# A decoder layer on one core: array shapes kept apart, GpSimd without arithmetic, softmax on turned scores

## The chip, the core and the metric

The kernel runs on one core of one Trainium2 chip. The metric is device microseconds of one execution. Three runs of the kernel before took 632.46, 633.56 and 633.76 us; their median is 633.56. A core has TensorE (matrix products), VectorE, ScalarE and GpSimd (elementwise work), and SyncE, which here issues all transfers. Each engine carries out its own instructions in the order in which the program lists them, and waits on semaphores for the others.

## The reference

One layer of a decoder for 512 tokens and 1024 channels. After an RMS norm, one projection gives the inputs of two token mixers and two merge gates. Branch A is causal attention with 8 heads of 64 channels and a relative-position bias (with 512 tokens every past block is selected, so all past keys count). Branch B is an RWKV-7 time mix, also 8 heads of 64 channels. The gated merge is followed by an output projection, a second RMS norm, and a gate that adds a per-layer embedding.

```python
u = _rms_norm(h, g_pre[i]);  cols = u @ w_in[i]
# A: softmax(q k' / 8 + bias[q_pos - k_pos], past keys only) @ v, times silu(z_A)
# B, for every token t and head (S is 64 x 64):
sa = einsum('bhvk,bhk->bhv', S, a_t)
S = S * w_t + sa b_t' + v_t k_t';   y_t = S r_t
# group norm of y, bonus, times silu(z_B)
merged = sigmoid(gate_a) * (y_a @ p_a) + sigmoid(gate_b) * (y_b @ p_b)
h = h + _rms_norm(merged @ w_out, g_post)
h = h + sigmoid(h @ w_ple_gate) * (p @ w_ple_up)
```

All inputs and the output are float32.

## The kernel before

Activations lie with channels on the 128 partitions and the 512 tokens along the free axis. A large product `w x` is made of three passes in the type float32r over a high and a low part of each operand: `wh xh + wh xl + wl xh`. Each pass is a TensorE instruction with a 128 x 128 weight tile and up to 512 columns; `product()` issues 24 of them for 8 tiles of input channels. Weights arrive in tiles of 128 x 1024 (`raw`). ScalarE makes the high part (`whi`), and VectorE or GpSimd subtracts it to make the low part (`wlo`); for the projections of the first phase every other tile goes to GpSimd (`weights()`, line 371).

The work has these stages. The start, to about 75 us, splits x, computes the norm and makes the first four projections. From then to about 480 us three things run at the same time. `fill()` makes the other projections in the order of the string `FILL`; its products are the `pp<-u_hi,whi` rows. `rwkv(j)` does the recurrence for four pairs of heads j one after the other: vectors and decays first, then the Gram products (`g<-W,BK`), the inverses of unit triangular matrices by doubling (`inverse()`, rows `Z`, `X`, `Xt`), and the chain over 8 chunks of 64 tokens. `attention()` does four pairs of heads: scores in `psc`, softmax, transposes in `ptp`, products with v. After that follow the merge, the output projection, the post-norm and the embedding gate.

Within the chain a chunk goes TensorE (`p_rhs`, rows `c<-SV,W`), ScalarE (`rh`), TensorE (`c<-rh,AT`), ScalarE or VectorE (`SV<-c`), TensorE (`p_s`), VectorE (`SV<-c,D,sd`), and so to the next chunk. The output `p_y` (rows `y<-SV,W`) is issued after the update. It has four products: for each of two heads one with 64 rows (`W1`, the old state) and one with 128 rows (`W2`, the new values), all with 64 weight columns. The head decides which half of the output partitions they write. The group norm of a pair ends with `y<-cst,Y`, which turns the result.

The scores (lines 1203 to 1207) take two products per head and query tile: `QS` with its high and low parts above each other on 128 rows times the high part `KH`, and the 64 rows with the high part of q times the low part `KL`. The up projections of decay and rate (lines 967 to 970) have the same form: 128 rows, then 64 rows with `wa_lo`. The softmax keeps two float16 parts of the probabilities (`ph`, `pl`), and the transposes are two float16 products per block of 128 x 128 against a scaled identity.

The order of instructions is not written out. The class `Plan` interleaves the streams at build time: every instruction is given a rough price in `Engine.price`, and the stream whose next step can start first goes on; recurrence and attention have a small bonus. So a price decides the order on every engine, and nothing at run time does. For TensorE the price is the number of columns with an allowance for the weight load, and 0.022 us for a product that runs beside its predecessor.

Of the kernel before, what the change touches and what calls it, by code (L numbers as in the profile page):

```python
# [35 lines left out]
T = 512  # L36
# [6 lines left out]
PSCALE = 16384.0  # L43
# [77 lines left out]
class Stream:  # L121
    """A sequence of instructions that yields the engine of its next step, or ("wait", mark)."""
# [101 lines left out]
class Engine:  # L224
    """An engine whose instructions are also priced in the plan."""
# [4 lines left out]

    def price(self, name, out, args, kw):
        """Microseconds, roughly."""
        n = math.prod((args[0] if name == "tensor_reduce" else out).shape[1:])
        if self.key == "P":
            m = args[0].shape[1]
            wide = out.dtype == F32 and args[0].dtype == F32
            four = args[0].dtype in (F32, F32R)
            load, d = ((4 * m, 4 * n) if wide else (2 * m, n) if four else (m // 4, n))
            load, d = max(0.0, load / 2400 - self.plan.streamed) if m > 64 else 0.0, d / 2400
            pos = out.base_partition() if m <= 64 else None  # L240
            beside = pos is not None and self.last is not None and pos != self.last
            self.last = None if beside else pos
            self.plan.streamed = 0.022 if beside else d
            return 0.022 if beside else load + d + 0.0025
# [34 lines left out]
class Queue:  # L279
    """The queue of the transfers, which are priced as well."""  # L280
# [15 lines left out]
def hybrid_kernel(ctx: ExitStack, tc, xT, pT, wu, wda, wmain, wpab, wout, wpg, vec_in, cst_in, oneh, relb, wupa,  # L296
# [47 lines left out]
    # weight tiles: their loads and splits run ahead of the products, those of the last two matrices in extra places  # L344
# [18 lines left out]
    def weights():  # L363
        for i, name in enumerate(order):
# [11 lines left out]
            eng = pool if i % 2 and name[0] not in "mow" else dve  # L376
# [12 lines left out]
    def product(name, ps, mh, ml, kts, cols=FULL, done=True, pace=None):  # L389
        """Adds w x over the k tiles kts = (of w, of x) on the given tokens."""  # L390
# [17 lines left out]
    def rsqrt(y, x, t):  # L408
        """y * RS = x ** -0.5 for x > 0: an integer seed, a step of Newton's kind and one of the third order."""
# [26 lines left out]
    def token_rstd(parts_, scale, eps, half, res):  # L436
        """[128, 256] of 1/sqrt(scale * column sums of the parts + eps), the same on every partition, in PSUM."""
# [30 lines left out]
    id16s = main.tile([128, 128], F16, name="id16s")  # L468
# [10 lines left out]
    # operands of the up projections of decay and rate, high and low parts above each other  # L479
    wd_x, ad_x, wd_w, ad_w, wa_lo = (main.tile([128, 512], F32R, name=n) for n in ("wd_x", "ad_x", "wd_w", "ad_w", "wa_lo"))  # L480
# [41 lines left out]
    def setup():  # L522
# [34 lines left out]
        dve.tensor_scalar(id16s, ident, 1.0 / PSCALE, None, op0=OP.mult)  # L557
# [27 lines left out]
    def first_split(i, q):  # L585
        ks = slice(2 * q, 2 * q + 2)
        yield ("wait", f"dw{i}")
        yield "A"
        act.activation(sw[i][0][:, ks], sraw[i][:, ks], AF.Copy)
        eng = pool if i or q else dve  # L590
        yield eng.key
        eng.tensor_tensor(sw[i][1][:, ks], sraw[i][:, ks], sw[i][0][:, ks].bitcast(F32), op=OP.subtract)
        plan.mark(f"f{i}{q}")

    def up_weights(w, there):
        plan.at(there)
        for a, b, d in ((lo_, hi_, wd_w), (hi_, lo_, ad_w)):
# [5 lines left out]
            dve.tensor_tensor(wa_lo[a], w[a], d[a].bitcast(F32), op=OP.subtract)  # L603
# [103 lines left out]
    def norm_split(kt, uf):  # L707
        yield "A"
        act.activation(u_hi[:, kt, :], uf, AF.Copy)
        yield "G" if kt % 2 else "D"  # L710
        (pool if kt % 2 else dve).tensor_tensor(u_lo[:, kt, :], uf, u_hi[:, kt, :].bitcast(F32), op=OP.subtract)
        plan.mark(f"u{kt}")

    def bias_lines():
        yield ("wait", "u7")
        for q in range(2):
# [3 lines left out]
            act.activation(line[:, 320 * q:320 * q + 320], ps[0:8, 0:320], AF.Copy)  # L720
# [12 lines left out]
    def statics():  # L733
        """The recurrence takes the place of the start."""
# [44 lines left out]
    def evacuate(i, w, j, ps):  # L779
# [15 lines left out]
        elif w == "Q":  # L795
            q = QS[j] = at.tile([128, 2, T], F32R, tag="qs", name="qs")
            for h, a, b in ((0, lo_, hi_), (1, hi_, lo_)):
                yield "A"
                act.activation(q[a, h, :], ps[a], AF.Copy, scale=0.125)
                dve.scalar_tensor_tensor(q[b, h, :], ps[a], 0.125, q[a, h, :].bitcast(F32), op0=OP.mult,  # L800
                                         op1=OP.subtract)
        elif w == "K":
            kh = KH[j] = at.tile([128, 2, T], F32R, tag="kh", name="kh")
            kl = KL[j] = at.tile([128, T], F32R, tag="kl", name="kl")
            for h, a, b in ((0, lo_, hi_), (1, hi_, lo_)):
# [3 lines left out]
                dve.tensor_tensor(kl[a, :], ps[a], kh[a, h, :].bitcast(F32), op=OP.subtract)  # L809
# [50 lines left out]
    def inverse(j, q, Ah, Al, AT, Xt, X):  # L860
        """The inverses of the unit triangular matrices of four chunks."""
# [74 lines left out]
    def rwkv(j):  # L936
# [8 lines left out]
        # 1 / |k * k_k| per token and head  # L945
# [18 lines left out]
        # log decays and in-context rates  # L964
        yield "P"
        pw, pa = bank(), bank()
        for ps, w, x, lo in ((pw, wd_w, wd_x, lo_), (pa, ad_w, ad_x, hi_)):
# [14 lines left out]
        # their sums from the middle of each chunk on, at 65 points; E = their exponentials  # L982
# [25 lines left out]
        # operands of the chunks: W1 = [a | L v part, r, identity, a of the second head], BK = [b, k]  # L1008
# [25 lines left out]
        def w1(eng, cs):  # L1034
# [500 lines left out]
```

## Time and profile before

| what | value |
|---|---|
| runs | 632.46, 633.56, 633.76 us |
| profiled execution, first to last instruction (the page gives no other time of it) | 635.5 us, 10491 instructions |
| TensorE, products | busy 615.8 us (97%), 3992 |
| TensorE, weight loads | 470.7 us (74%) |
| VectorE | 450.7 us (71%), 1003 |
| ScalarE | 310.2 us (49%), 695 |
| GpSimd | 105.5 us (17%), 87 |
| TensorE's mean granted clock | 0.983 |
| transfers | 64.51 MB, mean 102 GB/s |

The profile is of one execution. In its views PE is TensorE, PEld its weight loads, DVE VectorE, ACT ScalarE, POOL GpSimd. All instructions carry line 263, because one helper records them; the names of the tiles tell them apart (result first, then what is read). A matmul's duration includes its way through the array, so matmuls overlap and the distance from start to start is what one costs. A float32 product of 64 columns appears as two records.

### The profile page before, as it was taken

What the parts mean: (1) busy time and instruction counts of PE and PEld (TensorE: products, weight loads), DVE (VectorE), ACT (ScalarE), POOL (GpSimd) and SP (SyncE); (2) the same over time, 40 slices, a digit from 0 to 9 for tenths busy, and PEclk for the clock granted to TensorE, in tenths of its full rate; (3) what the DMA queues carried; (4) which work ended last, traced back from release to release, by engine and by line L of the source; (5) the groups of instructions that cost most, each with busy time, mean ns of one, the idle gap of its engine ahead of it and who ended that gap; (6) DMA issues with size and microseconds to landing.
All of it is one profiled execution on the core that took longest, in us unless ns stands there. A gap on an engine that the chain in (4) does not pass through costs nothing.

```text
span 635.5 us, 10491 instructions
## 1 busy us (share of the span) xinstructions
PE 615.8 (97%) x3992; PEld 470.7 (74%) x3992; DVE 450.7 (71%) x1003; ACT 310.2 (49%) x695; POOL 105.5 (17%) x87
## 2 busy tenths in 40 slices
PE   7999999999999999999999999999999999999997
PEld 4878777667776767676777666776778888898986
DVE  6987787876768878667977867675585766469533
ACT  7555264555455455446465354654463336444312
POOL 4531331101112110112111012201010001014100
PEclk9999999999999999799899999999999999999999
DMA  8315621112212121111210301221165555820211
GB/s 309 122 60 211 203 99 64 36 68 101 76 47 77 35 85 59 59 66 47 88 51 34 134 34 50 84 84 50 52 215 209 180 178 182 297 92 25 100 51 50
DMA packets 26210, 64.51 MB, mean 102 GB/s; under 512 B 2695, under 2 KB 7303, under 8 KB 25904
## 3 DMA queue, kind: packets, MB, share of 16 engines
q1 hardware_dynamic: 26160, 63.85, 28.8%
q8 instruction: 31, 0.51, 0.3%
q14 instruction: 19, 0.16, 0.1%
HBM read 55.69 MB, written 10.77 MB: 105 GB/s over the span
## 4 chain that ended last, share of the span: by engine, by line
PE 82%; DVE 13%; ACT 2%; issue 1%; DMA 1%; SPq 0%; DVEq 0%; ACTq 0%
PE pp L263 44%; PE s L263 12%; PE g L263 11%; PE c L263 8%; PE y L263 7%; DVE xl L263 2%; DVE BK L263 1%; DVE W L263 1%; DMA x_sb<-xT 1%; DVE tv L263 1%; DVE pr L263 1%; DVE xh L263 1%; DVE Y L263 1%; DVE mean L263 1%; DVE ph L263 0%
## 5 line engine op out<-in xcount | busy, mean ns | idle before, releaser
L263 PE MATMUL pp<-u_hi,whi 128*128 128x512 f32 x360 | 150.9, 419 | 0.0
L263 PE MATMUL pp<-u_hi,wlo 128*128 128x512 f32 x360 | 149.2, 414 | 0.0
L263 PE MATMUL pp<-u_lo,whi 128*128 128x512 f32 x360 | 148.4, 412 | 0.0
L263 POOL TENSOR_TENSOR wlo<-raw,whi 128x1024 fp32r<-128x1024 f32 (+1 forms) x29 | 60.5, 2093 | 319.2 <-ACT whi L263 313.4
L263 ACT ACTIVATE whi<-raw 128x1024 fp32r<-128x1024 f32 (+1 forms) x86 | 71.4, 846 | 30.9 <-PE pp L263 24.1
L263 PEld LDWEIGHTS pp<-u_hi,wlo 128*128 128x128 f32 x360 | 68.7, 191 | 15.0 <-issue 1.5
L263 PEld LDWEIGHTS pp<-u_lo,whi 128*128 128x128 f32 x360 | 68.7, 191 | 15.0 <-issue 2.0
L263 PEld LDWEIGHTS pp<-u_hi,whi 128*128 128x128 f32 x360 | 68.8, 191 | 14.2 <-issue 1.4
L263 DVE TENSOR_TENSOR wlo<-raw,whi 128x1024 fp32r<-128x1024 f32 (+1 forms) x57 | 52.8, 937 | 10.1 <-ACT whi L263 9.8
L263 PEld LDWEIGHTS y<-SV,W 64*64 64x64 f32 (+1 forms) x256 | 24.4, 134 | 15.6 <-issue 8.8
L263 PE MATMUL y<-SV,W 64*64 64x64 f32 (+1 forms) x256 | 35.4, 246 | 0.0
L263 ACT ACTIVATE rh<-c 128x64 f32<-128x64 f32 x29 | 6.5, 224 | 53.8 <-PE c L263 53.6
L263 ACT ACTIVATE SV<-c 64x64 f32<-64x64 f32 (+2 forms) x63 | 19.3, 306 | 23.0 <-DVE SV L263 14.0
L263 DVE SCALAR_TENSOR_TENSOR SV<-c,D,sd 64x64 f32<-64x64 f32 x56 | 15.8, 283 | 16.4 <-PE c L263 11.5
L263 PE MATMUL c<-SV,W 128*64 128x64 f32 x240 | 22.8, 243 | 3.6 <-ACT SV L263 2.9
L263 PEld LDWEIGHTS c<-SV,W 128*64 128x64 f32 x240 | 14.5, 136 | 15.1 <-ACT SV L263 8.2
L263 ACT ACTIVATE P<-P,sml 128x128 f32<-128x128 f32 (+3 forms) x32 | 17.9, 561 | 7.3 <-DVE sml L263 7.2
L263 PE MATMUL g<-W,BK 64*128 64x192 f32 x128 | 16.5, 360 | 4.2 <-DVE W L263 4.2
L263 DVE SCALAR_TENSOR_TENSOR pl<-P,sml,ph 128x128 f16<-128x128 f32 (+3 forms) x32 | 19.7, 615 | 1.1
L263 ACT ACTIVATE sd<-SV,D 64x64 f32<-64x64 f32 x56 | 19.1, 341 | 0.8
L263 PEld LDWEIGHTS g<-W,BK 64*128 64x128 f32 x128 | 11.7, 194 | 9.2 <-issue 8.9
L263 DVE CUSTOM_DVE_ANT_0 P<-s,bt 128x128 f32<-128x128 f32 (+3 forms) x32 | 15.5, 485 | 3.6 <-PE s L263 3.0
(372 smaller groups left out, 1401.3 us busy)
## 6 DMA issues: line engine op xcount, KB each, us to landing
raw<-wmain SPq DMA_DIRECT2D x48, 512.0 KB, 3.2
g_dram<-gst SPq DMA_DIRECT2D x16, 256.0 KB, 2.0
raw<-wpab SPq DMA_DIRECT2D x8, 512.0 KB, 3.3
raw<-wout SPq DMA_DIRECT2D x8, 512.0 KB, 3.7
raw<-wpg SPq DMA_DIRECT2D x8, 512.0 KB, 5.2
bb_dram<-b_dram SPq DMA_DIRECT2D x1, 2560.0 KB
x_sb<-xT SPq DMA_DIRECT2D x4, 512.0 KB, 5.0
bt<-bb_dram SPq DMA_DIRECT2D x8, 256.0 KB, 3.6
```

The costliest lines, as they stand in the source:

```text
L263: r = f(out, *args, **kw)
```

## The change

Three parts of it concern what TensorE is given. `KL` gets a second half: 128 rows with the low part of k on both halves, so that the second score product reads all 128 rows of `QS`. The up projections get low-part weights with 128 rows (`wd_l`, `ad_l`). The four products of `p_y` are issued in another order: first the two with 128 rows, one per head, then the two with 64 rows.

The planner's price for TensorE is replaced by `array()`. It knows the shape of the array that a product uses, and adds a price when the shape or the type changes.

GpSimd loses all its subtractions and products to VectorE (weight splits, `W1`'s second half, `yn`, `u_lo`, `h_lo`, `wul`, `pl` of the embedding); only memsets stay there. The softmax works on scores with the sign turned: q is scaled by -0.125 and the bias line by -1, the reduction takes a minimum, and the exponential has scale -1, so the negated maximum is there at once. The probabilities stay in float32 in `P`, the parts `ph` and `pl` go, and one float32 transpose takes the place of two float16 products. A scratch area for transfers issued elsewhere is made smaller.

```diff
 class Engine:
+    def array(self, name, out, w, n):
+        k, m = w.shape[0], math.prod(w.shape[1:])
+        if name == "transpose":
+            m = k
+        cut = lambda a: 32 if a <= 32 else 64 if a <= 64 else 128
+        mode, kind = (cut(k), cut(m)), w.dtype
+        each = lambda s: max(0.025, s / 2400 + 0.0025)
+        if kind == F32:
+            d = each(2 * n) if name == "transpose" else 2 * each(2 * n)
+        else:
+            d = n * 0.455e-3 if kind == F32R else each(n)
+        last = self.last
+        spot = w.base_partition(), out.base_partition()
+        full = (128, 128)
+        beside = lambda a, b: (mode[0] < 128 and a[0] != b[0]) or (mode[1] < 128 and a[1] != b[1])
+        if last is not None and last[0] == mode != full and all(beside(spot, s) for s in last[2]):
+            last[2].append(spot)
+            return 0.012
+        if last is not None and last[0] != mode:
+            d += 0.09 if last[1] == F32R else 0.045
+        if last is not None and kind == F32R and mode == full and (last[0] != full or last[1] != F32R):
+            d += 0.085
+        self.last = mode, kind, [spot]
+        self.plan.streamed = d
+        return d
...
-            eng = pool if i % 2 and name[0] not in "mow" else dve
+            eng = dve
...
-                act.activation(q[a, h, :], ps[a], AF.Copy, scale=0.125)
+                act.activation(q[a, h, :], ps[a], AF.Copy, scale=-0.125)
...
-            kl = KL[j] = at.tile([128, T], F32R, tag="kl", name="kl")
+            kl = KL[j] = at.tile([128, 2, T], F32R, tag="kl", name="kl")
...
-                dve.tensor_tensor(kl[a, :], ps[a], kh[a, h, :].bitcast(F32), op=OP.subtract)
+                dve.tensor_tensor(kl[a, h, :], ps[a], kh[a, h, :].bitcast(F32), op=OP.subtract)
+                yield "A"
+                act.activation(kl[b, h, :], kl[a, h, :].bitcast(F32), AF.Copy)
...
-            pe.matmul(ps, wa_lo[lo, jc], x[lo], start=False, stop=True)
+            pe.matmul(ps, low[:, jc], x, start=False, stop=True)
...
-                pe.matmul(p_y[lo_], W1[lo_, c, 1, :], SV[lo_, c, 0, 0, :], start=True, stop=False)
-                pe.matmul(p_y[lo_], W2[:, c, 0, 0:64], SV[:, c, 0, 1, :], start=False, stop=True)
-                pe.matmul(p_y[hi_], W1[hi_, c, 1, :], SV[hi_, c, 1, 0, :], start=True, stop=False)
-                pe.matmul(p_y[hi_], W2[:, c, 1, 0:64], SV[:, c, 1, 1, :], start=False, stop=True)
+                pe.matmul(p_y[lo_], W2[:, c, 0, 0:64], SV[:, c, 0, 1, :], start=True, stop=False)
+                pe.matmul(p_y[hi_], W2[:, c, 1, 0:64], SV[:, c, 1, 1, :], start=True, stop=False)
+                pe.matmul(p_y[lo_], W1[lo_, c, 1, :], SV[lo_, c, 0, 0, :], start=False, stop=True)
+                pe.matmul(p_y[hi_], W1[hi_, c, 1, :], SV[hi_, c, 1, 0, :], start=False, stop=True)
...
-        dve.tensor_tensor_reduce(P, psc, bt[:, T - n:T], 1.0, NEG, op0=OP.add, op1=OP.max, accum_out=mx)
-        dve.tensor_scalar(nm, mx, -1.0, None, op0=OP.mult)
+        dve.tensor_tensor_reduce(P, psc, bt[:, T - n:T], 1.0, -NEG, op0=OP.add, op1=OP.min, accum_out=nm)
...
-        act.activation(P, P, AF.Exp, bias=nm, accum_out=sm_)
+        act.activation(P, P, AF.Exp, bias=nm, scale=-1.0, accum_out=sm_)
...
-        dve.tensor_scalar(ri, ri, PSCALE, None, op0=OP.mult)
-        dve.tensor_scalar(ph, P, ri, None, op0=OP.mult)
-        dve.scalar_tensor_tensor(pl, P, ri, ph, op0=OP.mult, op1=OP.subtract)
+        dve.tensor_scalar(P, P, ri, None, op0=OP.mult)
...
-                        pe.matmul(psc[h][:, c], QS[j][rows, h, q], KL[j][rows, 0:n], start=False, stop=True)
+                        pe.matmul(psc[h][:, c], QS[j][:, h, q], KL[j][:, h, 0:n], start=False, stop=True)
...
-                        pe.matmul(ptp[h][:, c], ph[h][:, c], id16s, start=True, stop=False)
-                        pe.matmul(ptp[h][:, c], pl[h][:, c], id16s, start=False, stop=True)
+                        pe.transpose(ptp[h][:, c], P[h][:, c], ident)
```

## Rows read from the trace of the kernel before

**Rows 1.** The page: busy time, share of the span and instructions of each engine.
```profile
PE 615.8 (97%) x3992; PEld 470.7 (74%) x3992; DVE 450.7 (71%) x1003; ACT 310.2 (49%) x695; POOL 105.5 (17%) x87
```

**Rows 2.** The page: chain of work that ended last, shares of the span by engine.
```profile
PE 82%; DVE 13%; ACT 2%; issue 1%; DMA 1%; SPq 0%; DVEq 0%; ACTq 0%
```

**Rows 3.** TensorE's waits: who waited for whom, us in total, times, longest.
```profile
PE c L263 <- ACT SV L263: 2.9, 2, 1.5
```

**Rows 4.** Timeline of TensorE from 197 us (start, us, engine, what): score products.
```profile
197.06 0.33 PE L263 MATMUL s<-kh,qs 128*128 128x128 f32 x1
...
199.34 0.51 PE L263 MATMUL pp<-u_hi,whi 128*128 128x512 f32 x1
199.68 0.40 PE L263 MATMUL pp<-u_lo,whi 128*128 128x512 f32 x1
199.91 0.40 PE L263 MATMUL pp<-u_hi,wlo 128*128 128x512 f32 x1
```

**Rows 5.** Timeline of TensorE: y and the next chunk's first products.
```profile
175.79 1.04 PE L263 MATMUL y<-SV,W 64*64 64x64 f32 x7
...
176.94 0.50 PE L263 MATMUL pp<-u_lo,whi 128*128 128x512 f32 x1
```

**Rows 6.** Timeline of TensorE: a pair on 128 rows and 64 columns.
```profile
144.81 0.34 PE L263 MATMUL c<-SV,W 128*64 128x64 f32 x4
145.07 0.50 PE L263 MATMUL pp<-u_hi,wlo 128*128 128x512 f32 x1
```

**Rows 7.** Timeline of TensorE: eight pairs on 64 x 64, in brackets the wait before.
```profile
302.12 1.15 PE L263 MATMUL y<-cst,Y 64*64 64x64 f32 x32 [1.26 <-DVE Y L263]
303.20 0.51 PE L263 MATMUL pp<-u_lo,whi 128*128 128x512 f32 x1
```

**Rows 8.** Timeline of TensorE: the four up projections of one pair of heads.
```profile
79.20 0.40 PE L263 MATMUL g<-wd_x,wd_w 128*128 128x512 f32 x1
...
80.82 0.51 PE L263 MATMUL pp<-u_lo,whi 128*128 128x512 f32 x1
```

**Rows 9.** Timeline of TensorE: four float32 transposes.
```profile
296.81 0.60 PE L263 MATMUL pp<-cst,vc 128*128 128x128 f32 x4
297.24 0.49 PE L263 MATMUL c<-cst,vb 128*128 128x128 f32 x3
```

**Rows 10.** Timeline of TensorE: first and last of sixteen float16 products.
```profile
149.21 0.23 PE L263 MATMUL s<-id16s,ph 128*128 128x128 f16 x1
...
150.06 0.22 PE L263 MATMUL s<-id16s,pl 128*128 128x128 f16 x1
```

**Rows 11.** Groups by shape: busy us, mean ns, idle before; weight splits of both engines.
```profile
L263 POOL TENSOR_TENSOR wlo<-raw,whi 128x1024 fp32r<-128x1024 f32 x22 | 54.8, 2493 | 312.7 <-ACT whi L263 307.0 <-PE s L263 5.7
L263 DVE TENSOR_TENSOR wlo<-raw,whi 128x1024 fp32r<-128x1024 f32 x36 | 43.9, 1221 | 7.6 <-ACT whi L263 7.2
```

**Rows 12.** The page's costliest groups: the softmax's low part.
```profile
L263 DVE SCALAR_TENSOR_TENSOR pl<-P,sml,ph 128x128 f16<-128x128 f32 (+3 forms) x32 | 19.7, 615 | 1.1
```

**Rows 13.** Timeline of VectorE from 371 us.
```profile
372.46 2.77 DVE L263 TENSOR_TENSOR BK<-kka,En 128x512 f32<-128x512 f32 x1
375.15 0.68 DVE L263 TENSOR_TENSOR BK<-fk,En 128x512 f32<-128x512 f32 x1
```

**Rows 14.** Timeline of GpSimd, same stretch.
```profile
372.27 2.41 POOL L263 TENSOR_TENSOR wlo<-raw,whi 128x1024 fp32r<-128x1024 f32 x1 [23.02 <-ACT whi L263]
```

**Rows 15.** Timeline of TensorE, same stretch.
```profile
376.93 0.34 PE L263 MATMUL c<-SV,W 128*64 128x64 f32 x4 [1.51 <-ACT SV L263]
```

**Rows 16.** Busy time by stretch, granted clock third from last: first and last of three.
```profile
262.60:272.80 10.20, 10.20 (x28) 6.85 (x29) 5.14 (x10) 6.75 (x13) 0.00 (x0) 0.50 0.01 2
...
378.70:382.00 3.30, 3.30 (x14) 2.60 (x12) 1.04 (x3) 1.77 (x3) 0.00 (x0) 0.50 0.00 0
```

**Rows 17.** One tile's instructions: duration min/median/max in ns, first and last start.
```profile
L263 PE MATMUL y<-cst,Y x128: 218/218/267, 200.2 to 474.4; 64*64 64x64 f32 x128
```

**Rows 18.** Busy time by stretch (span, PE, PEld, DVE, ACT, POOL, clock), middle part.
```profile
75.00:475.00 400.00, 389.94 (x2777) 281.06 (x2776) 296.92 (x731) 210.37 (x498) 64.10 (x37) 0.98 0.20 70
```

More of the change, by code (lines that the diff above doesn't have):

```diff
@@ L42 @@
 GN_EPS = 64e-5
-PSCALE = 16384.0
 DECAY = math.exp(-0.5)
@@ L234, in price @@
         if self.key == "P":
[L235 to L244, printed above, removed]
+            return self.array(name, out, args[0], n)
         if name == "memset":
@@ L477, in shift_mix @@
         dve.scalar_tensor_tensor(o, ps, omu[:, col:col + 1], m[:, 0:T], op0=OP.mult, op1=OP.add)
-    wd_x, ad_x, wd_w, ad_w, wa_lo = (main.tile([128, 512], F32R, name=n) for n in ("wd_x", "ad_x", "wd_w", "ad_w", "wa_lo"))
+    wd_x, ad_x, wd_w, ad_w, wd_l, ad_l = (main.tile([128, 512], F32R, name=n)
+                                          for n in ("wd_x", "ad_x", "wd_w", "ad_w", "wd_l", "ad_l"))
     hw0 = main.tile([128, 4], F32, name="hw0")
@@ L589, in first_split @@
         act.activation(sw[i][0][:, ks], sraw[i][:, ks], AF.Copy)
-        eng = pool if i or q else dve
-        yield eng.key
-        eng.tensor_tensor(sw[i][1][:, ks], sraw[i][:, ks], sw[i][0][:, ks].bitcast(F32), op=OP.subtract)
+        yield "D"
+        dve.tensor_tensor(sw[i][1][:, ks], sraw[i][:, ks], sw[i][0][:, ks].bitcast(F32), op=OP.subtract)
         plan.mark(f"f{i}{q}")
@@ L596, in up_weights @@
         plan.at(there)
-        for a, b, d in ((lo_, hi_, wd_w), (hi_, lo_, ad_w)):
+        for a, b, d, low in ((lo_, hi_, wd_w, wd_l), (hi_, lo_, ad_w, ad_l)):
             yield "A"
@@ L602, in up_weights @@
             yield "D"
-            dve.tensor_tensor(wa_lo[a], w[a], d[a].bitcast(F32), op=OP.subtract)
+            for half in (a, b):
+                dve.tensor_tensor(low[half], w[a], d[a].bitcast(F32), op=OP.subtract)
         plan.mark("up")
@@ L709, in norm_split @@
         act.activation(u_hi[:, kt, :], uf, AF.Copy)
-        yield "G" if kt % 2 else "D"
-        (pool if kt % 2 else dve).tensor_tensor(u_lo[:, kt, :], uf, u_hi[:, kt, :].bitcast(F32), op=OP.subtract)
+        yield "D"
+        dve.tensor_tensor(u_lo[:, kt, :], uf, u_hi[:, kt, :].bitcast(F32), op=OP.subtract)
         plan.mark(f"u{kt}")
@@ L719, in bias_lines @@
             pe.matmul(ps[0:8, 0:320], rb_, oh[:, 320 * q:320 * q + 320], start=True, stop=True)
-            act.activation(line[:, 320 * q:320 * q + 320], ps[0:8, 0:320], AF.Copy)
+            act.activation(line[:, 320 * q:320 * q + 320], ps[0:8, 0:320], AF.Copy, scale=-1.0)
         sp.dma_start(b_dram, line)
@@ L966, in rwkv @@
         pw, pa = bank(), bank()
-        for ps, w, x, lo in ((pw, wd_w, wd_x, lo_), (pa, ad_w, ad_x, hi_)):
+        for ps, w, low, x in ((pw, wd_w, wd_l, wd_x), (pa, ad_w, ad_l, ad_x)):
             yield "P"
             pe.matmul(ps, w[:, jc], x, start=True, stop=False)
-            pe.matmul(ps, wa_lo[lo, jc], x[lo], start=False, stop=True)
+            pe.matmul(ps, low[:, jc], x, start=False, stop=True)
         Ep = rw.tile([128, NCH, 65], F32, name="Ep")
@@ L1032, in rwkv, with w1 @@
         ep3 = Ep[:, :, 1:65]
-        def w1(eng, cs):
-            yield "G" if eng is pool else "D"
-            eng.tensor_tensor(W1[:, cs, 1, :], r3[:, cs], ep3[:, cs], op=OP.mult)
-            yield "G" if eng is pool else "D"
-            eng.tensor_tensor(W1[lo_, cs, 0, :], kn3[lo_, cs], Ep[lo_, cs, 0:64], op=OP.mult)
-            yield "G" if eng is pool else "D"
-            eng.tensor_tensor(W1[hi_, cs, 3, :], kn3[hi_, cs], Ep[hi_, cs, 0:64], op=OP.mult)
+        def w1(cs):
+            yield "D"
+            dve.tensor_tensor(W1[:, cs, 1, :], r3[:, cs], ep3[:, cs], op=OP.mult)
+            yield "D"
+            dve.tensor_tensor(W1[lo_, cs, 0, :], kn3[lo_, cs], Ep[lo_, cs, 0:64], op=OP.mult)
+            yield "D"
+            dve.tensor_tensor(W1[hi_, cs, 3, :], kn3[hi_, cs], Ep[hi_, cs, 0:64], op=OP.mult)
             plan.mark(f"w1{j}.{cs.start}")
-        plan.spawn(w1(pool, slice(4, 8)), BR)
-        yield from w1(dve, slice(0, 4))
+        yield from w1(slice(0, 4))
+        plan.spawn(w1(slice(4, 8)), BR)
         yield "P"
@@ L1154, in rwkv @@
         yield ("wait", f"z{j}")
-        eng = pool if j < 3 else dve
-        yield eng.key
-        eng.tensor_tensor(yn, yn, bv, op=OP.add)
-        yield eng.key
-        eng.tensor_tensor(yn, yn, ZZ[j], op=OP.mult)
+        yield "D"
+        dve.tensor_tensor(yn, yn, bv, op=OP.add)
+        yield "D"
+        dve.tensor_tensor(yn, yn, ZZ[j], op=OP.mult)
         if j < 3:
@@ L1164, in rwkv, with softmax @@
         plan.mark(f"post{j}")
[L1166 to L1169 removed]
+    def softmax(h, P, psc, bt, n, name):
+        sml = at.tile([128, 3], F32, tag="sml", name="sml", bufs=4)
+        nm, sm_, ri = (sml[:, i:i + 1] for i in range(3))
         yield "D"
[L1171 to L1172 removed]
+        dve.tensor_tensor_reduce(P, psc, bt[:, T - n:T], 1.0, -NEG, op0=OP.add, op1=OP.min, accum_out=nm)
         yield "A"
[L1174 removed]
+        act.activation(P, P, AF.Exp, bias=nm, scale=-1.0, accum_out=sm_)
         yield "D"
         dve.reciprocal(ri, sm_)
[L1177 to L1179 removed]
+        dve.tensor_scalar(P, P, ri, None, op0=OP.mult)
         plan.mark(name)
@@ L1199, in attention @@
                 psc = [bank(f"s{h}", 1) for h in range(2)]
-                P, ph, pl = ([at.tile([128, T], d, tag=f"{t}{h}", name=t) for h in range(2)]
-                             for t, d in (("P", F32), ("ph", F16), ("pl", F16)))
+                P = [at.tile([128, T], F32, tag=f"P{h}", name="P") for h in range(2)]
                 for h, rows in heads:
@@ L1409, in h_split @@
         act.activation(hi[:, n, c], x[:, n, c], AF.Copy)
-        yield "G" if n % 2 else "D"
-        (pool if n % 2 else dve).tensor_tensor(lo[:, n, c], x[:, n, c], hi[:, n, c].bitcast(F32), op=OP.subtract)
+        yield "D"
+        dve.tensor_tensor(lo[:, n, c], x[:, n, c], hi[:, n, c].bitcast(F32), op=OP.subtract)
         plan.mark(f"h{n}.{h}")
```

20 lines of the change are left out of this document (7 added, 13 removed).

## The prediction

> **What bounds the kernel now.** I began with the page's busy shares: TensorE is busy for 97% of the span [rows 1], and the chain that ended last gives it 82% and VectorE 13% [rows 2]. A busy TensorE is not yet one that streams, since matmuls overlap, so the next view was its timeline, read from start to start. Between two large products of 512 columns with nothing else around the starts lie 0.23 us apart, as at 199.68 and 199.91 [rows 4]. That is 0.45 ns a column, and it is the yardstick for all that follows: what a stretch takes above it is the cost of something other than streaming. Two such costs stand out. Whenever a product uses another part of the array than the one before it (64 rows or 64 columns in place of 128), the starts move apart [rows 4 to 8]. And VectorE is sometimes held for two microseconds beside a GpSimd instruction, after which TensorE waits [rows 13 to 15]. The waits as such are short: 2.9 us in all for the chain's products [rows 3], 1.26 us for one group norm [rows 7]. So from about 75 us on the kernel is bound by what TensorE is given to do, with the recurrence, whose norms come 91 us apart (four bursts from 200.2 to 474.4) [rows 17], as a serial path beside it that is nearly as long.
>
> **Low parts of the scores on 128 rows.** The eight score products of two heads run from 197.06 to 199.34, that is 2.28 us, for 2 x 2 x (128 + 256) = 1536 columns, which stream in 1536 x 0.45 = 0.69 us [rows 4]. The excess of 1.59 us belongs to the four products with 64 rows: 0.40 us each, for going to the other shape and back. With `KL` on 128 rows the shape doesn't change, and the streaming stays as it is (columns count, not rows). There are 4 pairs x 2 heads x 4 query tiles = 32 of them: 12.7 us. From below I set half of it (6.4), should a short product of 128 columns not reach the yardstick. On this the Trainium skill has a rule in "TensorE: Matmul & The Clock Gate", section LDWEIGHTS: loading weights takes the number of their columns divided by 1.2, about 107 ns for 128, and by its section on weight-path modes float32 gets no faster path. By that rule the 16 products with 128 columns (0.06 us of streaming) would last some 0.05 us longer each, an estimate from that page, and the sum would be 0.8 us higher; no row of before has such a product between others of its own shape.
>
> The copies that fill the second half of `KL` are 8 ScalarE instructions of 64 x 512. ScalarE is busy 49% [rows 1]; they delay a pair's first scores by well under a microsecond and I cost them at nothing, 0 to 2.4 us if scores were what ended a stage.
>
> **Up projections on 128 rows.** Four products take 79.20 to 80.82 = 1.62 us, where four of 512 columns stream in 0.92 [rows 8]: 0.70 us, once for each of 4 pairs, 2.8 us. The two additional subtractions come once, early, on VectorE: below 1.5 us, and not waited for there.
>
> **y in pairs of heads.** Now a chunk's four products change shape each time: with the next chunk's first product pair behind them they take 175.79 to 176.94 = 1.15 us [rows 5]. Afterwards they are three pairs, each in one shape. A pair on 128 rows and 64 columns takes 0.26 us with the change behind it [rows 6]. Of a pair on 64 x 64 eight in a row take 1.08 us, 0.14 each [rows 7]; alone it is between this and the 0.26 of the other pair, and I take 0.26, because it too is followed by a change. 3 x 0.26 = 0.78, so 0.37 us are saved, in 32 chunks 11.8 us. Ends: 0.25 to 0.50 a chunk (8 to 16 us).
>
> **Float32 transposes.** Four existing ones go from 296.81 to 297.24, 0.11 us each [rows 9]. What they replace: 16 float16 products in 15 steps from 149.21 to 150.06, 0.057 us each, two to a block [rows 10], so 0.113. Nothing, in 80 blocks, give or take 1 us. Signs turned in scale factors cost nothing.
>
> **No arithmetic on GpSimd.** Its 105.5 us [rows 1] go to VectorE, which does the same split of 128 x 1024 in 1.22 us instead of 2.49 [rows 11]: about half, some 51 us. VectorE loses the 19.7 us of `pl` [rows 12] and 64 short instructions. What it also loses are the holds: `BK<-kka,En` takes 2.77 us where a like instruction right behind takes 0.68 [rows 13], while GpSimd is in a 2.41 us split [rows 14]; the chain's update stood behind it, and TensorE then waited 1.51 us [rows 15]. Each of the 22 splits there [rows 11] can hold one instruction for 2.77 - 0.68 = 2.1 us, which is 0 to 46 us; I take half, 23, of which some 20 fall between 75 and 475 us. So 51 - 20 - 23 - the short ones leaves next to nothing: VectorE, busy 297 of these 400 us [rows 18], should stay near that.
>
> The granted clock was at its lower level, 1.2 GHz, in three stretches, the first of 10.2 and the last of 3.3 us [rows 16], some 16.8 us together, of which half is lost: 8.4 us. Before each of them TensorE had just waited 1.3 to 1.5 us, the last two times as in rows 7 and 15. With the waits (2.9 + 1.3) there are 12.6 us that hang on held instructions. VectorE's order stays strict, and a split can still stand before the chain; I take 8 of them (0 to 12.6).
>
> **The order.** The planner prices TensorE anew, by shape changes that the trace shows, so all engines get a new order, and every queue's instructions move against each other. It cannot be read from the profile. Each return to the large products costs 0.34 instead of 0.23 us, as from 199.34 to 199.68 [rows 4]; with 70 interruptions more or fewer, a guess at a third of them, that is 8 us either way, and I take nothing. The transfers are issued by SP as before; the smaller scratch space for transfers issued elsewhere costs nothing.
>
> **Sum.** 12.7 + 2.8 + 11.8 + 8 = 35.3; 635.5 - 35.3 = 600.2. The profiled execution is 1.9 us above the median of the runs, which would make 598. Can the recurrence follow? It must lose 35.3 / 4 = 8.8 us in each of its 91 us. It has 8 x 0.37 = 3.0 from y, which stands before the next chunk's product; up to 20 / 4 = 5.0 from holds; some of the 3.2 from the scores that it queues behind; 2 from the clock. With two thirds of that, 9, it just does. For this narrow margin I leave the 2 us in and say 600, with 590 to 610 as this case's own range.
>
> **Rivals.**
> 1. The recurrence becomes the bound. For: it is serial, and nearly as long as TensorE's work now. Against: TensorE hardly waits for it now [rows 3]. If it gains only the y pairs and the up projections, 3.7 us a period, 14.8 in all, the time is 635.5 - 14.8 = 621, whatever TensorE saves.
> 2. The new order interrupts the large products more often, 140 times rather than 70: 140 x 0.11 = 15 us, so 615. For: nothing in the change makes the planner prefer to stay in a shape; it only prices the change. Against: priced right, it fits fewer products into gaps that are too short.
> 3. The change doesn't do what it says: the excess comes from short products, not from the shape. Then y gives nothing, the scores 6.4, the up projections 2.8, the waits 4: 622. Against: 512 columns on 64 rows pay as much [rows 8].
> 4. Slower: VectorE's strict order. The 22 splits of 1.22 us that come from GpSimd [rows 11] stand before the chain's updates. One that does costs up to 1.2 us of waiting, and if the clock falls after it, as it did after rows 15, 1.7 us more: 2.9. The 27.3 us saved in TensorE's work are used up from the tenth on; with 16 it is 635.5 - 27.3 + 46.4 = 655. For: an update that waited behind one long instruction is what rows 13 to 15 show. Against: 36 of these splits run on VectorE already [rows 11], and the long waits came beside GpSimd.
>
> **How the numbers follow.** Forecast 0.60, rivals in order 0.16, 0.10, 0.07, 0.07. The likeliest gives 600. Upwards the range goes to 620, which takes in the second rival and half of the first; downwards to 584, where y gives 16, all 12.6 us come back and the order helps by some 7. Rival 4 and the rest of 1 and 3 stay outside, about two in ten. 0.2% is 1.3 us, about what a measurement of this kernel tells from no change: faster 0.91, within it 0.02, slower 0.07.
>
> **What would show it.** Right: score products of one shape at the yardstick (two heads of the first group in 0.7 to 0.9 us), a y group in 0.5, up projections in 0.9; no VectorE instruction of 512 elements above 1.5 us; less than 5 us at the lower clock after the start; norms 80 to 84 us apart. Wrong: TensorE waits for `SV` or `rh` that add up to over 15 us (rivals 1 and 4), more returns to the large products at the same saving within the groups (2), or groups that keep their old length (3).

## The result, and the profile after

The changed kernel takes 605.33 us (median of four runs, 604.81 to 606.52) against 633.66 us beside it: ratio 0.953 (95% interval 0.950 to 0.957), 28.3 us faster. Its profiled execution has a span of 604.7 us where before had 635.5, so 30.8 us are to be found between the two traces. Two later runs of the same kernel gave 605.27 and 603.98 us.

First the page: busy time, share of the span and instructions of each engine, and the chain that ended last [rows 1, 2].

```profile
PE 584.1 (97%) x3912; PEld 456.0 (75%) x3912; DVE 431.0 (71%) x989; ACT 313.1 (52%) x698; POOL 1.5 (0%) x11
...
PE 82%; DVE 9%; ACT 6%; DMA 2%; issue 1%; SPq 0%; ACTq 0%; DVEq 0%
```

TensorE sets the pace as before and is busy for 31.7 us less. VectorE has not become busier for the work that it took over: 450.7 us before, 431.0 now. The gain lies in the middle part, here with the columns of [rows 18] (stretch, its length, busy time of PE, PEld, DVE, ACT, POOL, the granted clock): 400 us before, 370 now.

```profile
75.00:445.00 370.00, 360.85 (x2695) 266.27 (x2695) 277.85 (x678) 214.42 (x502) 0.00 (x0) 1.00 0.24 78
```

TensorE's timeline shows the three kinds of groups that the change touches. The first of eight score products, and the large products behind them [rows 4]:

```profile
196.58 0.22 PE L280 MATMUL s<-kh,qs 128*128 128x128 f32 x1
196.64 0.27 PE L280 MATMUL s<-kl,qs 128*128 128x128 f32 x1
196.75 0.34 PE L280 MATMUL s<-kh,qs 128*128 128x256 f32 x1
...
197.50 0.40 PE L280 MATMUL pp<-u_hi,wlo 128*128 128x512 f32 x1
197.74 0.39 PE L280 MATMUL pp<-u_hi,whi 128*128 128x512 f32 x1
```

Eight products take 0.92 us where they took 2.28, and the large product behind them costs its ordinary 0.24 us, not 0.34. The y group and the next chunk's first pair [rows 5, 6]:

```profile
165.31 0.60 PE L280 MATMUL y<-SV,W 128*64 128x64 f32 x8
165.83 0.34 PE L280 MATMUL c<-SV,W 128*64 128x64 f32 x4
166.10 0.50 PE L280 MATMUL pp<-u_hi,whi 128*128 128x512 f32 x1
```

They take 0.79 us in place of 1.15. The four up projections [rows 8] take 0.93 us in place of 1.62:

```profile
80.25 0.39 PE L280 MATMUL g<-wd_x,wd_w 128*128 128x512 f32 x1
...
81.18 0.40 PE L280 MATMUL pp<-u_lo,whi 128*128 128x512 f32 x1
```

The float32 transposes [rows 9, 10], eight of them and what follows, take 228.63 - 227.76 = 0.87 us, 0.109 each:

```profile
227.76 1.03 PE L280 MATMUL s<-cst,P 128*128 128x128 f32 x8
228.63 0.33 PE L280 MATMUL c<-rh,AT 128*128 128x64 f32 x2
```

The instruction on VectorE that had been held for 2.77 us [rows 13] now takes the same time in all four pairs (one tile's instructions: least, median and greatest duration in ns, first and last start):

```profile
L280 DVE TENSOR_TENSOR BK<-kka,En x4: 673/692/693, 88.8 to 351.7; 128x512 f32<-128x512 f32 x4
```

The weight splits that came from GpSimd run on VectorE at its own price [rows 11]; and the norms of the four pairs come (445.2 - 191.3) / 3 = 84.6 us apart in place of 91.4 [rows 17]:

```profile
L280 DVE TENSOR_TENSOR wlo<-raw,whi 128x1024 fp32r<-128x1024 f32 x58 | 70.8, 1221 | 11.8 <-ACT whi L280 11.3
```
```profile
L280 PE MATMUL y<-cst,Y x128: 218/218/267, 191.3 to 445.2; 64*64 64x64 f32 x128
```

What did not get better are TensorE's waits (who waited for whom, us in total, times, longest) [rows 3]:

```profile
PE s L280 <- DVE wlo L280: 4.1, 2, 2.3
PE pp L280 <- DVE wlo L280: 1.8, 1, 1.8
PE pp L280 <- ACT vc L280: 1.4, 1, 1.4
PE s L280 <- ACT whi L280: 1.4, 1, 1.4
PE c L280 <- ACT SV L280: 1.2, 3, 0.6
```

They add up to 16.0 us (all lines of the view), against 15.5 before; two later executions of the same kernel show 14.4 and 15.2. The waits for the recurrence (`W`, `SV`, `Y`: 9.1 us before, 3.0 now) have given way to waits for weight splits, now VectorE's. Two of them end at 11 and 17 us, at the start (4.1 us), another stands at 437 us. The chain of waits there (start, us, what) shows what the split stood behind on VectorE: first work on a branch output, whose transfer takes 3.94 us of the chain, then the end of a pair's group norm:

```profile
428.36 3.94 DMA yf<-yB_dram
...
432.32 1.25 ACT yh L280 x2
...
436.05 0.18 DVE var L280
...
436.25 0.04 DVE rstd L280
...
436.33 1.24 DVE wlo L280
...
437.61 6.71 PE pp L280 x21
```

Both places have a lower clock (third column from the end) behind them [rows 16]:

```profile
17.99:21.40 3.41, 3.41 (x19) 3.41 (x18) 3.40 (x8) 2.44 (x7) 0.00 (x0) 0.50 0.77 267
...
437.90:441.20 3.30, 3.30 (x9) 2.53 (x9) 3.20 (x9) 1.41 (x2) 0.00 (x0) 0.50 0.79 210
```

In the two later executions the wait at the second place was 1.0 and 1.2 us, and the clock did not fall there.

The account from start to start on TensorE, summed over all groups of a kind in each trace (a group lasts until the start of the next instruction outside it):

| us | before | after | difference |
|---|---|---|---|
| score products | 22.8 | 10.8 | -12.0 |
| up projections | 7.6 | 4.1 | -3.5 |
| y and the pair behind it | 36.6 | 24.2 | -12.4 |
| TensorE's waits, all | 15.5 | 16.0 | +0.5 |
| at 1.2 GHz behind 30 us, half of it lost | 17.1 | 3.4 | -6.9 |
| at 1.2 GHz in the first 30 us, half of it lost | 3.4 | 6.8 | +1.7 |

The groups give 27.9, but 3.4 us of that stand twice: 1.5 us by which two groups of before are longer at the lower clock, and two of its waits, 1.3 us behind a score group and 0.7 us within a y group. 27.9 - 3.4 - 0.5 + 6.9 - 1.7 = 29.2 of the 30.8 us.

The clock's part differs between executions. The time lost to it, (1 - mean granted clock) x span, is 10.8 us in the profiled execution of before, but 7.5 to 8.5 us on the average of its runs beside the experiments, and 3.9 to 5.3 us in the runs of after. So on the runs' average the clock gives 2 to 4 us and not 6.9 - 1.7 = 5.2.

### The profile page after: what moved, and what is told of

Read it like the earlier page. It is cut to its first block, busy times and chain, and to the rows that moved or that the text cites. A ratio compares the mean times of both kernels' runs of the same rounds, so it can differ in the third digit from the quotient of the medians.

```text
span 604.7 us, 10216 instructions
## 1 busy us (share of the span) xinstructions
PE 584.1 (97%) x3912; PEld 456.0 (75%) x3912; DVE 431.0 (71%) x989; ACT 313.1 (52%) x698; POOL 1.5 (0%) x11
## 4 chain that ended last, share of the span: by engine, by line
PE 82%; DVE 9%; ACT 6%; DMA 2%; issue 1%; SPq 0%; ACTq 0%; DVEq 0%
PE pp L280 46%; PE s L280 12%; PE g L280 11%; PE c L280 8%; PE y L280 5%; DVE rn L280 1%; ACT whi L280 1%; ACT kh L280 1%; DVE wlo L280 1%; DMA x_sb<-xT 1%; DVE W L280 1%; DVE xl L280 1%; DMA yf<-yB_dram 1%; ACT SV L280 1%; DVE SV L280 0%
## 5 line engine op out<-in xcount | busy, mean ns | idle before, releaser
L280 PE MATMUL pp<-u_hi,whi 128*128 128x512 f32 x360 | 149.1, 414 | 0.0
L280 DVE TENSOR_TENSOR wlo<-raw,whi 128x1024 fp32r<-128x1024 f32 (+1 forms) x86 | 81.4, 960 | 12.3 <-ACT whi L280 11.8
L280 PEld LDWEIGHTS c<-SV,W 128*64 128x64 f32 x240 | 12.0, 134 | 15.4 <-ACT SV L280 8.6
L280 PEld LDWEIGHTS y<-SV,W 128*64 128x64 f32 (+1 forms) x256 | 13.2, 133 | 12.1 <-issue 8.3
L280 PE MATMUL c<-SV,W 128*64 128x64 f32 x240 | 20.0, 245 | 1.9 <-ACT SV L280 1.2
L280 PE MATMUL y<-SV,W 128*64 128x64 f32 (+1 forms) x256 | 19.7, 244 | 0.0
L280 DVE TENSOR_TENSOR W<-g,cst 64x128 f32<-64x128 f32 (+1 forms) x64 | 17.2, 290 | 0.8
L280 ACT ACTIVATE gst<-pp 128x512 f32<-128x512 f32 x16 | 9.5, 597 | 15.3 <-PE pp L280 15.1
L280 PE MATMUL pp<-m_hi,wlo 128*128 128x512 f32 (+1 forms) x48 | 17.1, 357 | 0.0
L280 PE MATMUL pp<-m_lo,whi 128*128 128x512 f32 (+1 forms) x48 | 17.1, 356 | 0.0
```

The source lines that it names most:

```text
L280: r = f(out, *args, **kw)
```

## Experiments

Each ran beside the kernel before on the same chip (634.97 to 635.04 us there). Differences are between medians; those to after are to the 605.27 us from the chip of the first three (the others ran on two more chips). Three questions: does the price of a change of shape explain the three groups; what did GpSimd cost; and what is the new order worth.

**The kernel after, twice more**, as the measure for the others: 605.27 us (0.955) and 603.98 (0.951).

> The changed kernel once more, to have it on the same chip as the three that follow. Both theories: 605 us.

> The changed kernel again, beside the next one on the same chip. All theories: 605 us.

**One part undone, with the order of all else kept.** In the first three the plan is that of after and only what is issued differs.

`e1_y_apart`: y head by head.

```diff
-                pe.matmul(p_y[lo_], W2[:, c, 0, 0:64], SV[:, c, 0, 1, :], start=True, stop=False)
-                pe.matmul(p_y[hi_], W2[:, c, 1, 0:64], SV[:, c, 1, 1, :], start=True, stop=False)
-                pe.matmul(p_y[lo_], W1[lo_, c, 1, :], SV[lo_, c, 0, 0, :], start=False, stop=True)
-                pe.matmul(p_y[hi_], W1[hi_, c, 1, :], SV[hi_, c, 1, 0, :], start=False, stop=True)
+                # the four of before, in their sequence
```

> The changed kernel, with the four products of y in the old sequence (64 rows, 128 rows, 64, 128) and every other instruction of every engine in the same order. Theory (TensorE's work sets the time, a shape change costs what the start-to-start distances say): the y groups took 36.6 us in the kernel before and take 24.2 now, so about 12 us come back, 617. Rival (something beside TensorE sets the pace, and y lies in gaps): at most 3 us come back, 608 or less.

Measured: 615.05 us, 0.969 (0.967 to 0.972), 9.8 us above after. In its trace y and the pair behind it take 35.6 us, 11.4 more than in after. Its timeline of TensorE has the old pattern, each product 0.25 us behind the other, 166.19 - 165.94:

```profile
165.94 0.33 PE L1143 MATMUL y<-SV,W 64*64 64x64 f32 x2
166.19 0.33 PE L1144 MATMUL y<-SV,W 128*64 128x64 f32 x2
166.45 0.33 PE L1145 MATMUL y<-SV,W 64*64 64x64 f32 x2
```

9.8 / 32 = 0.31 us a chunk: four small products cost by their sequence alone.

`e2_rows64`: low parts of scores and up projections on 64 rows.

```diff
-            pe.matmul(ps, low[:, jc], x, start=False, stop=True)
+            nc.tensor.matmul(ps, low[rs, jc], x[rs], start=False, stop=True)
...
-                        pe.matmul(psc[h][:, c], QS[j][:, h, q], KL[j][:, h, 0:n], start=False, stop=True)
+                        nc.tensor.matmul(psc[h][:, c], QS[j][rows, h, q], KL[j][rows, h, 0:n], start=False, stop=True)
```

> The changed kernel, with the low parts of the scores and of the up projections multiplied on 64 rows, as before, and every instruction of every engine in the same order. Theory: 32 products at 0.40 us and 4 times 0.70 us come back, 15.5 us, 621; of this 13 to 16 as the two traces' groups have it. Rival (hidden): 608 or less. A third one, that short products and not the shape were slow: the scores don't change, 3 us from the up projections, 608.

Measured: 617.45 us, 0.974 (0.971 to 0.978), 12.2 us above after. In its trace the scores take 21.2 us and the up projections 6.6, together 12.9 more than in after; the account's 12.0 + 3.5 hold 2.4 us of a wait and of lower clock. Its timeline of TensorE shows the same columns streaming on half the rows; two heads take 2.17 us again:

```profile
200.01 0.22 PE L281 MATMUL s<-kh,qs 128*128 128x128 f32 x1
200.16 0.32 PE L1227 MATMUL s<-kl,qs 64*128 64x128 f32 x1
200.42 0.38 PE L281 MATMUL s<-kh,qs 128*128 128x256 f32 x1
...
202.18 0.50 PE L281 MATMUL pp<-u_hi,wlo 128*128 128x512 f32 x1
```

`e3_splits_pool`: every other weight split of the first phase back on GpSimd.

```diff
-                dve.tensor_tensor(lo[:, c], raws[i][:, c], hi[:, c].bitcast(F32), op=OP.subtract)
+                (nc.gpsimd if i % 2 and name[0] not in "mow" else nc.vector).tensor_tensor(
+                    lo[:, c], raws[i][:, c], hi[:, c].bitcast(F32), op=OP.subtract)
```

> The changed kernel, with every other weight split of the first phase back on GpSimd, planned as if on VectorE, so that all other instructions keep their order. Theory (GpSimd holds VectorE, the chain's updates come late, TensorE waits and its clock falls): stretched VectorE instructions of over 2 us are back, 5 to 13 us more, 610 to 618. Rival (VectorE's strict queue is what matters, and it gets rid of 22 splits of 1.22 us): nothing or a gain, 600 to 606.

Measured: 618.8 us, 0.975 (0.972 to 0.978), 13.5 us above after, a little over the range of the theory. TensorE's waits rise from 16.0 to 24.6, and the time lost to the lower clock by 3.8 us, (1 - 0.986) x 617.0 against (1 - 0.992) x 604.7: together 12.4, where the spans differ by 12.3. Fourteen instructions of VectorE run at least 0.7 us longer than the median of their kind, 21 us in all; after has none, before thirteen, 22 us in all. The one here has 8 elements a partition and takes 0.17 us in the other three pairs; GpSimd is in a split meanwhile (timelines of VectorE and of GpSimd):

```profile
261.96 2.04 DVE L281 TENSOR_SCALAR mean<-mean 128x8 f32<-128x8 f32 x1
...
261.57 2.40 POOL L404 TENSOR_TENSOR wlo<-raw,whi 128x1024 fp32r<-128x1024 f32 x1 [20.93 <-ACT whi L281]
```

TensorE's waits in that kernel: what comes late are again vectors of the recurrence, while the waits for `wlo` itself do not rise (5.0 us, 5.9 in after).

```profile
PE y L281 <- DVE Y L281: 2.7, 3, 2.3
PE g L281 <- DVE rb L281: 2.4, 2, 1.7
```

`e4_old_price`: all work of after, planned with TensorE's price of before.

```diff
-            return self.array(name, out, args[0], n)
+            ...  # load + columns, as before
```

> The changed kernel, planned with the old price of TensorE; the work is the same, the order is not. Theory (the new prices are neutral within what an order is worth): 605 plus or minus 8, 597 to 613. Rival (the new prices, by packing products of one shape, are a main part of the gain): 618 or more, with more returns to the large products than the 196 of the changed kernel.

Measured: 612.61 us, 0.966 (0.962 to 0.969), 7.3 us above after. Products `pp<-u` that follow other work are 200 against 193 (187 before), which at 0.11 us explains under one microsecond. (The 196 and 225 of the expectations also count returns within the score groups and up projections, which the change itself takes out.) Its first 30 us have the clock at 0.77 where after has 0.89 and before 0.94, the same columns as above:

```profile
0.00:30.00 30.00, 22.98 (x114) 18.53 (x114) 20.97 (x53) 18.08 (x46) 0.83 (x8) 0.77 0.67 225
```
```profile
0.00:30.00 30.00, 23.02 (x128) 19.14 (x129) 21.89 (x64) 19.03 (x47) 0.83 (x8) 0.89 0.65 223
```

(0.89 - 0.77) x 30 = 3.6 us, about half of the 7.3. This differs between executions, for e1 and e2 have the start of after and show 0.83; but over all its runs e4 has a mean granted clock of 0.985 and after one of 0.991 to 0.994, which is 4 to 5 us. The rest stays open.

**One part alone, on the kernel before.** Its work, its prices and its order stand unless the edit says otherwise.

`e5_new_price`: the price alone.

```diff
-            return load + d + 0.0025
+            return self.array(name, out, args[0], n)
```

> The kernel before, planned with the new price of TensorE and nothing else changed. Theory: 634 plus or minus 8, 626 to 642. Rival (prices are a main part): 622 or less, with fewer returns to the large products than the 225 of the kernel before.

Measured: 664.78 us, 1.046 (1.043 to 1.050): 30 us slower, outside both forecasts. Products `pp<-u` behind other work are 192 (187 before), so it isn't interruptions. TensorE's waits are 33.5 us. The first two pairs of the recurrence get ahead, with norms at 189.0 and 271.7 us (200.2 and 302.1 before). But the projections fall behind: 473 products `pp<-u` have begun by 240 us, 553 before. So the third pair's input `kb` arrives at 278.5 us, in the kernel before at 241.2, after at 244.0 (timelines of VectorE, this kernel's, then before's and after's), and that pair's norm comes at 411.0 us (392.6 before).

```profile
278.52 0.75 DVE L281 SCALAR_TENSOR_TENSOR kb<-pp,omu,mix 128x512 f32<-128x512 f32 x1 [4.35 <-ACT mix L281]
```
```profile
241.17 0.75 DVE L263 SCALAR_TENSOR_TENSOR kb<-pp,omu,mix 128x512 f32<-128x512 f32 x1 [0.93 <-ACT mix L263]
```
```profile
244.03 0.75 DVE L280 SCALAR_TENSOR_TENSOR kb<-pp,omu,mix 128x512 f32<-128x512 f32 x1 [2.33 <-ACT mix L280]
```

`e6_shapes`: the three groups in one shape, in the order of before.

```diff
-            pe.matmul(ps, wa_lo[lo, jc], x[lo], start=False, stop=True)
+            nc.tensor.matmul(ps, low[:, jc], x, start=False, stop=True)
...  # scores and y likewise, as in the change; low parts copied to 128 rows
```

> The kernel before in its own order, with only the shapes changed: low parts of scores and up projections on 128 rows, y in pairs; GpSimd, softmax, transposes and prices stay. Theory (TensorE's work sets the time): 25 to 27 us less, 607 to 611, with GpSimd's holds and the lower clock still there. Rival 1 of the prediction (the recurrence sets the pace): 15 us less, 620 or more, with longer waits of TensorE for the chain.

Measured: 626.84 us, 0.988 (0.985 to 0.990): 8.2 us faster, where the theory had 25 to 27. The groups shrink by some 23 us all the same, while TensorE's waits rise from 15.5 to 28.3, 21.0 of them for the recurrence (`W`, `SV`, `X`, `rh`, `Y`). The chain that ended last gives TensorE 65% and VectorE 23% of the span, where before had 82% and 13%:

```profile
PE g L264 <- DVE W L264: 5.7, 5, 2.0
PE c L264 <- DVE SV L264: 5.0, 3, 3.1
PE c L264 <- ACT SV L264: 3.4, 2, 2.0
```

`e7_no_pool`: GpSimd's arithmetic issued on VectorE, in the place that it had in the order of before.

```diff
-        f = getattr(self.real, name)
+        f = getattr(self.aside if self.aside is not None and name != "memset" else self.real, name)
...
+    pool.aside = nc.vector
```

> The kernel before with all of GpSimd's arithmetic issued on VectorE at the same place of the plan, priced as on GpSimd, so that the order is kept. Theory (holds): 5 to 13 us less, 621 to 629, no VectorE instruction of 512 elements above 1.5 us, less time at the lower clock. Rival 4 of the prediction (VectorE's strict order): 51 us more work on VectorE with nothing taken from it by the softmax, 640 or more.

Measured: 632.76 us, 0.996 (0.993 to 0.999): 2.3 us faster, less than the 5 to 13 of the theory, and nowhere near rival 4's 640. In the profiled execution no instruction is held, and the clock doesn't fall behind the first 30 us (over its ten runs the mean granted clock is 0.987 to 1.000). But TensorE's waits rise to 19.0, 8.2 of them for `W`; that they come from the splits which VectorE now has among the recurrence's work is likely, but was not traced.

`e8_shapes_no_pool`: the edits of e6 and e7 together. By then I held that two bounds lie close together, TensorE's work and a recurrence that GpSimd holds up, so that both edits are needed for either to count.

> The kernel before in its own order, with the shapes changed as in the run of shapes alone and GpSimd's arithmetic issued on VectorE at the same place of the plan; softmax, transposes and prices stay. Theory (two bounds close to each other: shapes relieve TensorE, the end of GpSimd's holds relieves the recurrence, and each shows only with the other): far more than the 8.2 + 2.3 us of the two alone, 25 to 30 us, 605 to 610. Rival (they simply add, and the rest is the planner's new order): 622 to 626.

Measured: 627.66 us, 0.988 (0.985 to 0.991): no faster than e6 alone. That theory fell. The groups are 21 us shorter, nothing is held, and TensorE waits 33.4 us, 24.0 of them for the recurrence; the chain that ended last gives it 64% and VectorE 21%:

```profile
PE g L265 <- DVE W L265: 9.0, 9, 1.4
PE c L265 <- DVE SV L265: 5.5, 5, 3.1
PE c L265 <- ACT rh L265: 2.8, 1, 2.8
```

So in the order of before the recurrence sets the pace as soon as TensorE gets faster, with GpSimd or without. What frees it in the changed kernel, its other order or its shorter softmax on VectorE, these runs do not tell apart.

`e9_price_no_pool`: the edits of e5 and e7 together.

> The kernel before planned with the new price, GpSimd's arithmetic issued on VectorE at the same place of that plan. Theory (the new price's 30 us loss comes from GpSimd: splits that come late and hold VectorE, which no price knows): most of it goes, 632 to 642. Rival (the order itself is poor with the old shapes): 655 or more.

Measured: 651.64 us, 1.026 (1.023 to 1.030). It lies between the two forecasts. Of the 30 us that the price alone costs, 13 go with GpSimd's arithmetic; the remaining 17 stay, and the third pair's `kb` still comes only at 273.7 us.

**An attempt to do better.** `x2_start_pool_late_y`: the first weight splits again on GpSimd, to take the 4.1 us of waits off the start, and the branch outputs planned 2.5 us later, for the split at 437 us.

```diff
-        dve.tensor_tensor(sw[i][1][:, ks], sraw[i][:, ks], sw[i][0][:, ks].bitcast(F32), op=OP.subtract)
+        eng = pool if i or q else dve
+        eng.tensor_tensor(sw[i][1][:, ks], sraw[i][:, ks], sw[i][0][:, ks].bitcast(F32), op=OP.subtract)
...
-        plan.at(there)
+        plan.at(there + 2.5)
```

> The changed kernel with two edits that its trace suggests: the first four weight tiles are split on GpSimd as before (TensorE waited 4.1 us for these splits on VectorE), and the plan takes the transfers of the branch outputs to land 2.5 us later (ScalarE waited for them in front of a weight split at 435 us, and TensorE 1.8 us after it). Theory: 2 to 5 us less than the changed kernel, 600 to 603. Rival (GpSimd holds the splits of x at the start for as long as it saves): no less, 604 to 607.

Measured: 603.91 us, 0.952 (0.949 to 0.955), where after on the same chip took 603.98: nothing is gained. Of the waits for `wlo` 0.8 us are left, and others have come in their place, at the start above all:

```profile
PE s L280 <- ACT whi L280: 2.5, 1, 2.5
PE s L280 <- DVE xl L280: 2.2, 6, 0.5
PE pp L280 <- ACT vc L280: 1.4, 1, 1.4
```

## Why the prediction was right, and where it was not

The forecast was 600 us, the measurement 605.3. By its steps:

- **Scores, up projections and y** (12.7 + 2.8 + 11.8 = 27.3): right in mechanism, and 2.8 us too large. Without what stands twice the account has 10.7 + 2.4 + 11.4 = 24.5. The scores came short most, 10.7 for 12.7: their products still take 10.8 us where their 20480 columns would stream in 9.2. The mechanism is shown, not argued: e1 and e2 put back the shape changes alone, in a kept order, and pay 9.8 and 12.2 us. A y group with its next pair took 0.79 us where 0.78 were worked out. Rival 3 is out.
- **Short products of one shape**, which no row of before had: of two products of 128 columns the first takes 0.06 us (196.58 to 196.64), as its columns stream, the second 0.11 (to 196.75), and the one of 256 columns behind them 0.17 (to 196.92), where 0.12 would stream. The starts of their weight loads lie 0.11 to 0.12 us apart:

```profile
196.58 0.19 PEld L280 LDWEIGHTS s<-kl,qs 128*128 128x128 f32 x1
196.69 0.19 PEld L280 LDWEIGHTS s<-kh,qs 128*128 128x128 f32 x1
196.80 0.19 PEld L280 LDWEIGHTS s<-kl,qs 128*128 128x128 f32 x1
```

  By the Trainium skill ("TensorE: Matmul & The Clock Gate", section LDWEIGHTS) a load takes the number of its columns divided by 1.2, about 107 ns for 128. These starts agree with it. The delay does not fall on each short product, as the prediction had it, but its two places make 0.05 us each for eight heads, so the 0.8 us that its sum left out came.
- **Waits and clock** (8): the step that was mis-sized. The clock's part came behind the start (6.9 of 8.4 us), but 1.7 went back at the start, and the waits stayed at 16 us, since splits on VectorE now stand before what TensorE needs. 4.7 came in place of 8 between the two traces, and less on the runs' average, as the clock gave 2 to 4 us there. This is rival 4's mechanism in small; the places are the start and 437 us, where the split stands behind a branch output and the norm, and not the norm behind the split. The prediction also compared a span with times: wherever the record has both for one execution, the time is 1.7 to 2.1 us above the span. So the profiled execution of before was some 3.7 us slower than the median, not 1.9, and a span of 600.2 is a time of 602.
- **Transposes** (0): right, 0.109 us a block where 0.113 stood.
- **VectorE near its old load**: held as a share of the span, 71% in both. 51 us of GpSimd's work were to come, and yet VectorE's busy time fell by 19.7, with the softmax's low part, short instructions and the holds gone; the holds of before were 22 us where 23 were taken. And e3 gives the price of GpSimd's part from the other side: 13.5 us when the splits go back, more than the 8 that the prediction put on all waits and clock. In the order of before (e7) taking all arithmetic off GpSimd gives 2.3. That such splits cost more in a faster kernel is likely, but the two moves are not the same, and it is not shown.
- **The order** (0, give or take 8): the step that was wrong. It was sized by interruptions of the large products, and these hardly moved (`pp<-u` behind other work: 187 before, 193 after, so rival 2 is out too). The runs point to another measure, what the recurrence and its inputs get from an order: the same savings on TensorE give 8 us in the old order (e6, e8), where the whole change with its own plan gives 28, and the new price alone goes from 7 us gained with the new work (e4 to after) to 30 lost with the old (e5). On the changed work the two prices lie within the 8 us, but not by the mechanism that gave the 8.
- **Can the recurrence follow** (8.8 us a period wanted, 9 estimated): it got 6.8, and TensorE hardly waits for it (`W`, `SV`, `rh`, `X`, `Y`: 4.5 us; before 9.1). Rival 1 was the right fear for a kernel that keeps its order: e6 gives 626.8 where it said 621.
- **The signs**: y groups in 0.52 us, up projections in 0.93, no VectorE instruction of 512 elements above 1.5 us and 3.4 us at the lower clock after the start came as forecast; two heads in 0.92 us and norms 84.6 us apart lie just outside (0.9 and 84).

So the time came out near the forecast with TensorE's terms right within 3 us, the waits and the clock too large by 3 us, and an order that served the recurrence. This last was luck: nothing in the prediction said that it would, and with the old order the same savings gave 8 us. The parts don't add: put back one at a time they cost 9.8 + 12.2 + 13.5 + 7.3 = 42.8 us of a total of 30; alone on the kernel before they give 8.2 and 2.3 and cost 30.

Open are the 15 us between e8 (627.7) and e4 (612.6): both have the new shapes and the old price, but e4 also has the new softmax and transposes, and a plan made for the changed work; these two were not run apart. In the traces a difference of that size lies in TensorE's waits, 33.4 us against 17.6; which edit takes them away is not known. Why the new price alone costs 30 us is seen in part (two pairs get ahead, the projections behind, and the third pair waits for its input) but not traced to one decision of the planner.

## What to carry to other kernels

Measure products from start to start, and look for the stretches above the rate of the large ones: work that goes back and forth between array shapes pays at each step, and can be regrouped at little cost (here 8 copies and 2 subtractions). Where instructions stand in a fixed order, a saving on the busiest engine is worth only what the next chain allows in that order, here a third; plan anew with the work as it will be, and test a price together with the work it was made for. A split moved off an engine that gets in others' way must still be placed: what it waits behind is the next thing to look at, though moving two such waits away gained nothing here (x2).

## What the runs showed of the hardware

- A hold by GpSimd hits the smallest instructions too: 8 elements a partition took 2.04 us instead of 0.17 beside a split of 2.40 us (e3).
- The clock fell to 1.2 GHz for 3.3 us after a wait of 1.8 us at 437 us, and not in two later executions, where the wait there was 1.0 and 1.2 us. In the first 30 us it stood at 1.2 GHz for 6.8 us (3.4 in before, 13.7 in e4). The profiled execution of e7, with 19.0 us of waits in all, kept 2.4 GHz behind its start: the sum of the waits doesn't tell it.
- Going to products on 64 rows and back costs time of its own: in e2, with the order kept, scores and up projections take 12.9 us more for the same columns.
